# Memory attention of a transformer layer put into a written order, with the pre-norm weights in the folded keys

## The chip, the cores and the metric

The kernel runs on one core of a Trainium2 chip. The metric is the device time of one execution in microseconds (us). Before the change it is 1554.91 us (median of 3 runs, 1554.90 to 1556.88).

The core has five engines with a queue each: TensorE (PE: matrix products and transposes), VectorE (DVE), ScalarE (ACT), GpSimd (POOL) and SyncE (SP, which here issues the DMA transfers). Each engine works through its queue strictly in order, and waits on semaphores for the others. PE writes its results into PSUM, in which a tile of this kernel takes one bank. The banks go by four tags ("mm", "s", "tr", "pv") of two banks each.

## The reference, cut to what matters

```python
h = rmsnorm(x, g_mix_pre);  proj = h @ w_in                      # queries, keys, values, forget gates
y_fox = forgetting_attention(...); y_chk = chunked_relpos_attention(...)
y = concatenate([rmsnorm(y_fox, g_fox_out), rmsnorm(y_chk, g_chk_out)])
x = x + rmsnorm(y @ w_out, g_mix_post)                           # mixing
h = rmsnorm(x, g_mem_pre);  mem_n = rmsnorm(mem, g_mem_kv)
k = mem_n @ w_mk;  v = mem_n @ w_mv                              # 4 heads of 256, 256 memory tokens
p = softmax((h @ w_mq) k^T / 16)                                 # per head
x = x + rmsnorm((p v) @ w_mo, g_mem_post)                        # memory attention
h = rmsnorm(x, g_ff_pre)
x = x + rmsnorm(square(relu(h @ w_ff1)) @ w_ff2, g_ff_post)      # feed-forward, hidden 4096
```

There are 1024 rows of x, 1024 columns, everything is float32, and `rmsnorm(a, g)` divides a row by the root of its mean square (plus 1e-6) and multiplies by the weights g.

## The kernel before, in words

Products. A float32 product is made of three matmuls in a faster format (`mm3`, L102 to L104): each operand is split into a rounded part `hi` and the rest `lo`, and hi*hi, hi*lo and lo*hi are summed in PSUM. A weight block is loaded by DMA into a raw tile (`wraw`, three buffers), then split: `whi` by a copy on ACT (L96), `wlo` by a subtraction on DVE or POOL (L97). Activations are split in the same way when they are copied out of PSUM after a transpose (`to_T`: four transposes L127, `hi` on ACT L140, `lo` on DVE L141).

Tiling. Rows come in 8 blocks of 128 (`n`, or `b` within one half), the two halves of 512 rows are called `th`, the two halves of 512 output columns `nh`. A result of 128 rows by 512 columns sums 1024 products in 24 matmuls, or 512 products in 12.

Folding. The query and key projections of the memory attention are multiplied into one matrix ahead of time (`fold_keys`: `w_mq` of a head times the keys of that head, scaled by 1/16 at L460 and L462, stored to DRAM), so that scores are `h` times the folded keys. Likewise `fold_values` multiplies the memory values with `w_mo` (results `fv`, copied by L478 on DVE and L480 on ACT, stored to DRAM), so that the output is the probabilities times the folded values. Folded matrices are loaded back as weight blocks.

Stages around the change, in the order of time:
- End of attention (about 480 to 560 us). The last heads of the chunked attention run beside the memory keys (`mem_side`, `mkm`) and the folded keys (`fk`). In the same stretch `head_outputs(th, 0)` works on group 0 of the head outputs (the forgetting heads): load from DRAM (`oin`), `yT_hi` on ACT (L563), `yT_lo` on DVE (L564), squares on ACT (L567 to L570), sums of squares on DVE (L571, L572).
- Memory values (`mvm`, evacuated by `vm_hi` L442 and `vm_lo` L443) and the first half of the output projection, `mix_out((0, 1), 0)`: results `yw`, evacuated by L627 on ACT with the head's inverse root as scale. `head_rstd` makes that root from the summed squares by 4 small matmuls (`ssh`), DVE and POOL (L592).
- The second half of the output projection, `mix_out`, once for each `th`, with the weights loaded for each. A result is added (L629, DVE), squared with a sum for the row (`square_sum`, L597, ACT), and multiplied by the post-norm weights (L631, DVE). `close_block` then makes the inverse root of a row (L109 on DVE, L111 and L112 on POOL), adds the residual x (L673, DVE), stores the row, squares it (ACT), makes the next root and multiplies by that root and `g_mem_pre` (L678, DVE). `fold_values` runs in two parts between these.
- The transposes of the normed rows (`h2T`), scores, softmax (maximum L702 DVE, exponentials L704 ACT, reciprocal L706 DVE, scaling L709 POOL) and the transposed probabilities (`mtr` L712, `oT_hi` L715, `oT_lo` L716), for each `th` and each pair of heads: `cross`.
- The output of the memory attention (`ym`): `mem_out` for the first 512 columns, `row_tile` for the second. For `th` = 0 rows are closed as above with the names h3; the transposes of `h3T` lie in the middle of `mem_out` of `th` = 1 (`meanwhile`).
- The feed-forward: its weights are split ahead (`split_ahead`, `whi_a` L824, `wlo_a` L827), POOL makes eight sums `xf` (L894) of the parts of `h3T`, and the rows of `th` = 1 are closed one behind the other (`row_out`, `row_sum` L972, `row_norm` L979), then transposed (`trx` L914).

What sets the order. Up to the last stage the instructions of each engine are put in order by a scheduler, from the program's order, its own estimates of duration and the buffers. From `manual = ExitStack()` on, with `tc.manual_schedule()`, each engine gets its instructions in the order in which the program writes them. Before the change that begins at the last four row tiles.

Of the kernel before, what the change touches and what calls it, by code (L numbers as in the profile page):

```python
# [13 lines left out]
F32 = mybir.dt.float32  # L14
# [30 lines left out]
def build(ctx, tc, nc, out, t):  # L45
# [115 lines left out]
    gcol = const.tile([P, KC], F32, name="gcol")  # L161

# [271 lines left out]
    def mem_side(mT, src, name):  # L434

        act = Act(name, NM)
        for nb in range(KC):
            wh, wl = load_w(t[src][nb], [P, KC, P], lo_on=lo_eng())
            ps = mm_tile([P, NM], f"m{name}{nb}")
            for kc in range(KC):  # L440
                mm3(ps, wh[:, kc, :], wl[:, kc, :], mT.hi(kc), mT.lo(kc), kc == 0, kc == KC - 1)
            nc.scalar.activation(act.hi(nb), ps, AF.Copy)  # L442
            nc.vector.tensor_sub(act.lo(nb), ps, f(act.hi(nb)))  # L443
# [21 lines left out]
    def fold_values(vm, nhs):  # L465

        for nh in nhs:
            for h in range(4):
                wh, wl = load_w(row_pair(t["w_mo"], h, nh), [P, 2, HT], lo_on=lo_eng())
                g = u4(f"fvs{h}{nh}", (P, 2, HT), F32)  # L470
                for m in range(2):
                    ps = mm_tile([P, HT], f"fv{h}{nh}{m}")
                    ms = slice(m * P, (m + 1) * P)
                    for d in range(2):
                        mm3(ps, vm.hi(h * 2 + d, ms), vm.lo(h * 2 + d, ms), wh[:, d, :], wl[:, d, :],
                            d == 0, d == 1)
                    if m:
                        nc.vector.tensor_copy(g[:, m, :], ps)  # L478
                    else:
                        nc.scalar.activation(g[:, m, :], ps, AF.Copy)  # L480
                nc.sync.dma_start(vd_d[h][nh], g)
# [43 lines left out]
    nc.sync.dma_start(gcol, t["g_heads"])  # L525
    bias_rows()
# [24 lines left out]
    def head_outputs(th, g):  # L551
# [4 lines left out]
        for i in range(2):  # L556
            o = u4(f"oin{th}{g}{i}", (P, 2, HT), F32)
            for j in range(2):
                kc = g * 4 + i * 2 + j
                nc.sync.dma_start(o[:, j, :], od[kc][th])  # L560
                gc = gcol[:, kc:kc + 1]
                dh = yh[i][:, j, :]
                nc.scalar.activation(dh, o[:, j, :], AF.Copy, scale=gc)  # L563
                nc.vector.scalar_tensor_tensor(yl[i][:, j, :], o[:, j, :], gc, f(dh),  # L564
                                               op0=ALU.mult, op1=ALU.subtract)
# [9 lines left out]
    parts = {(th, 0): head_outputs(th, 0) for th in range(2)}  # L575
    fold_keys(mem_side(mT, "w_mk", "km"))
# [26 lines left out]
    PAIRS = ((0, 1), (2, 3))  # L603

    def mix_out(ths, g, after=None):

        rs = {}
        for nh in range(2):
            cs = slice(nh * HT, (nh + 1) * HT)
            ws = [load_w(row_pair(t["w_out"], 2 * g + i, nh), [P, 2, HT], u4 if g and nh else None,  # L610
                         lo_eng()) for i in range(2)]
            for th in ths:
                yh, yl, sq = parts[th, g]
                y, ss = ys[th]
                for b in range(4):
                    c = slice(b * P, (b + 1) * P)
                    ps = mm_tile([P, HT], f"yw{th}{g}{nh}{b}")
# [4 lines left out]
                    if th not in rs:  # L622
                        rs[th] = head_rstd(th, g, sq)
                    r = rs[th][:, b:b + 1]
                    yc = y[b][:, cs]
                    if g == 0:
                        nc.scalar.activation(yc, ps, AF.Copy, scale=r)  # L627
                    else:
                        nc.vector.scalar_tensor_tensor(yc, ps, r, yc, op0=ALU.mult, op1=ALU.add)  # L629
                        square_sum(yc, ss[b][:, nh:nh + 1], HT)  # L630
                        nc.vector.tensor_tensor(yc, yc, gpost[:, cs], op=ALU.mult)  # L631
            if after and nh in after:
                after[nh]()

    def o_at(o, b, kc):
        h, l = o[kc // 4][b // 2]
# [3 lines left out]
    def mem_out(th, o, y, ss, g, nhs=(0, 1), hook=lambda kp: None):  # L640


        for nh in nhs:
            cs = slice(nh * HT, (nh + 1) * HT)
            ps = [mm_tile([P, HT], f"ym{th}{nh}{b}", "mm" if b < 2 else "s") for b in range(4)]
            for kp in range(4):
                wh, wl = load_w(vd_d[kp][nh], [P, 2, HT], lo_on=lo_eng())
                for b in range(4):
                    for j in range(2):
                        mm3(ps[b], *o_at(o, b, kp * 2 + j), wh[:, j, :], wl[:, j, :],  # L650
                            kp == 0 and j == 0, kp == 3 and j == 1)
                hook(kp)
            for b in range(4):
                square_sum(ps[b], ss[b][:, nh:nh + 1], HT)
                nc.vector.tensor_tensor(y[b][:, cs], ps[b], g[:, cs], op=ALU.mult)

    def row_tile(o, b, wo, name, tag):

        ps = mm_tile([P, HT], name, tag)
        for kp in range(4):  # L660
            for j in range(2):
                mm3(ps, *o_at(o, b, kp * 2 + j), wo[kp][0][:, j, :], wo[kp][1][:, j, :],
                    kp == 0 and j == 0, kp == 3 and j == 1)
        return ps

    def close_block(y, ss, th, xin, xout, gnext, nm, bs):

        for b in bs:
            tb = th * 4 + b
            xt = p2.tile([P, D], F32, tag="xt", bufs=2, name=f"xt{nm}{tb}")  # L670
            nc.sync.dma_start(xt, xin(tb))
            r = rstd_of(ss[b], f"{nm}y{tb}")
            nc.vector.scalar_tensor_tensor(xt, y[b], r, xt, op0=ALU.mult, op1=ALU.add)  # L673
            nc.sync.dma_start(xout(tb), xt)
            s2 = small.tile([P, 1], F32, tag="ss", bufs=8, name=f"s2{nm}{tb}")
            square_sum(xt, s2)
            r = rstd_of(s2, f"{nm}x{tb}")
            nc.vector.scalar_tensor_tensor(y[b], xt, r, gnext, op0=ALU.mult, op1=ALU.mult)  # L678

    def turn(y, th, act, nm, pairs=PAIRS):  # L680
        for a, b in pairs:
            to_T(y[a], y[b], act, a * P, f"{nm}{th}{a}")

    def cross(th, act, after=None):

        o = []
        for nh in range(2):
            ps = [mm_tile([P, HT], f"ms{th}{nh}{b}", "mm" if b < 2 else "s") for b in range(4)]
            for kp in range(4):
                wh, wl = load_w(kd_d[kp][nh], [P, 2, HT], lo_on=lo_eng())  # L690
                for b in range(4):
                    c = slice(b * P, (b + 1) * P)
                    for j in range(2):
                        mm3(ps[b], act.hi(kp * 2 + j, c), act.lo(kp * 2 + j, c), wh[:, j, :], wl[:, j, :],
                            kp == 0 and j == 0, kp == 3 and j == 1)
            o.append([(u4(f"oT_hi{th}{nh}{i}", (P, 4, 2 * P)), u4(f"oT_lo{th}{nh}{i}", (P, 4, 2 * P)))
                      for i in range(2)])
            for b in range(4):
                st = small.tile([P, 6], F32, tag="mst", bufs=4, name=f"mst{th}{nh}{b}")
                pr = p2x.tile([P, 2, NM], F32, tag="mp", bufs=4, name=f"mp{th}{nh}{b}")  # L700
                sc = ps[b].rearrange("p (h m) -> p h m", h=2)
                nc.vector.tensor_reduce(st[:, 0:2], sc, axis=mybir.AxisListType.X, op=ALU.max, negate=True)  # L702
                for h in range(2):
                    nc.scalar.activation(pr[:, h, :], sc[:, h, :], AF.Exp, bias=st[:, h:h + 1],  # L704
                                         accum_out=st[:, 2 + h:3 + h])
                nc.vector.reciprocal(st[:, 4:6], st[:, 2:4])  # L706
                tr = mm_tile([P, 4, P], f"mtr{th}{nh}{b}", "tr")
                for h in range(2):
                    nc.gpsimd.tensor_scalar(pr[:, h, :], pr[:, h, :], st[:, 4 + h:5 + h], 1.0,  # L709
                                            op0=ALU.mult, op1=ALU.mult)  # L710
# [711 lines left out]
```

## Time and profile before

| | |
|---|---|
| Median of 3 runs | 1554.91 us |
| The profiled execution | 1553.97 us, of which the span from the first to the last instruction is 1552.2 us |
| PE (matmuls and transposes) busy | 1504.1 us, 97% of the span |
| DVE busy | 946.2 us, 61% |
| ACT busy | 796.5 us, 51% |
| POOL busy | 379.6 us, 24% |
| Mean granted PE clock | 0.993 |

Rows of the profile name the line, the engine, the operation and its operands as output<-input with the program's names; then come the count, the busy time with the mean duration in ns, and the idle time before with what ended it. A row of the waits tells which instruction ended PE's idle time: us in total, times, and the longest. A row of the timeline gives the start in us and the duration. Matmuls are pipelined, so that their mean duration is longer than the distance from one to the next.

### The profile page before, as it was taken

To read this page: it belongs to the slowest core of one execution; us is meant where nothing else is said; L and a number is where in the kernel's file an instruction comes from. 1 tells how busy PE (TensorE), PEld (TensorE's weight loads), DVE (VectorE), ACT (ScalarE), POOL (GpSimd) and SP (SyncE) were. 2 spreads that over 40 slices of the span, in tenths; PEclk is the share of its full clock that TensorE was granted. 3 is DMA by queue.
4 is the path that set the end of the run, shared out by engine and by line. 5 is a ranking of instruction groups with operands and counts; after the bars stand their busy time and mean duration, and the time that the engine had idled before them with its cause. 6 is when DMAs were issued, how large, how long until landed. Compare 5 with 4: busy or idle time off the path is not lost.

```text
span 1552.2 us, 22221 instructions
## 1 busy us (share of the span) xinstructions
PE 1504.1 (97%) x7948; PEld 1276.3 (82%) x7948; DVE 946.2 (61%) x1612; ACT 796.5 (51%) x1409; POOL 379.6 (24%) x546
## 2 busy tenths in 40 slices
PE   8999999999998999999999989999999999999998
PEld 7978889789877998777888877888888888888886
DVE  6366574665467763478655568766555474746577
ACT  5356564565466663545454445555555544444442
POOL 4234351343233440002220250443323000000021
PEclk9999999999999899999999999999999999999999
DMA  5132140242223375267524454775444595535565
GB/s 214 50 95 65 52 113 23 76 146 64 55 65 128 93 236 195 82 217 257 190 82 139 147 176 139 249 250 189 155 151 149 185 390 192 174 109 195 198 244 190
DMA packets 90640, 237.49 MB, mean 153 GB/s; under 512 B 10505, under 2 KB 18705, under 8 KB 90530
## 3 DMA queue, kind: packets, MB, share of 16 engines
q1 hardware_dynamic: 90530, 236.08, 45.7%
q8 instruction: 63, 1.03, 0.3%
q14 instruction: 47, 0.39, 0.1%
HBM read 168.35 MB, written 59.30 MB: 147 GB/s over the span
## 4 chain that ended last, share of the span: by engine, by line
PE 84%; DVE 6%; ACT 3%; DMA 3%; issue 2%; POOL 2%; SPq 0%; DVEq 0%; POOLq 0%; ACTq 0%
PE fx L103 4%; PE fx L104 4%; PE fx L102 3%; PE fy L104 3%; PE fy L103 3%; PE fy L102 3%; PE px L104 3%; PE px L103 3%; PE px L102 3%; PE ms L104 2%; PE ms L103 2%; PE ms L102 2%; PE v L102 2%; PE pz L103 2%; PE pz L104 2%
## 5 line engine op out<-in xcount | busy, mean ns | idle before, releaser
L96 ACT ACTIVATE whi<-wraw 128x1024 fp32r<-128x1024 f32 x92 | 96.8, 1057 | 97.0 <-PE ms L104 29.2
L97 DVE TENSOR_TENSOR wlo<-wraw,whi 128x1024 fp32r<-128x1024 f32 x68 | 84.3, 1244 | 75.0 <-ACT whi L96 74.5
L1149 ACT ACTIVATE whif<-ra 128x1024 fp32r<-128x1024 f32 x37 | 39.2, 1060 | 122.4 <-PE fy L103 62.6
L1151 DVE TENSOR_TENSOR wlof<-ra,whif 128x1024 fp32r<-128x1024 f32 x37 | 45.3, 1225 | 91.2 <-ACT whif L1149 91.2
L1265 POOL TENSOR_SCALAR rf<-sf 128x1 f32<-128x1 f32 x8 | 8.3, 1036 | 326.4 <-ACT jf L1250 326.1
L102 PE MATMUL v<-whiv,hT_hi 128*128 128x256 f32 (+1 forms) x256 | 73.7, 288 | 0.8 <-DVE vs L238 0.8
L103 PE MATMUL v<-wlov,hT_hi 128*128 128x256 f32 (+1 forms) x256 | 73.4, 287 | 0.0
L104 PE MATMUL v<-whiv,hT_lo 128*128 128x256 f32 (+1 forms) x256 | 73.2, 286 | 0.0
L97 POOL TENSOR_TENSOR wlo<-wraw,whi 128x1024 fp32r<-128x1024 f32 x24 | 58.1, 2422 | 48.0 <-ACT whi L96 26.9
L103 PE MATMUL fx<-vlof,whif 128*128 128x512 f32 x168 | 65.4, 389 | 0.0
L102 PE MATMUL fx<-vhif,whif 128*128 128x512 f32 x168 | 65.4, 389 | 0.0
L104 PE MATMUL fx<-vhif,wlof 128*128 128x512 f32 x168 | 65.4, 389 | 0.0
L1039 POOL TENSOR_TENSOR sc<-wf,wf 128x512 f32<-128x512 f32 x14 | 21.2, 1513 | 143.5 <-DMA wf<-in_w_ff 127.2
L102 PE MATMUL yw<-whi,yT_hi 128*128 128x512 f32 x128 | 50.4, 397 | 2.6 <-ACT yw L627 1.4
L102 PE MATMUL ym<-whi,oT_hi 128*128 128x512 f32 x128 | 49.6, 402 | 3.0 <-DVE h3T_lo L141 3.0
L103 PE MATMUL yw<-wlo,yT_hi 128*128 128x512 f32 x128 | 50.2, 393 | 1.7 <-DVE wlo L97 1.7
L103 PE MATMUL ym<-wlo,oT_hi 128*128 128x512 f32 x128 | 50.8, 397 | 0.0
L104 PE MATMUL ym<-whi,oT_lo 128*128 128x512 f32 x128 | 50.7, 396 | 0.0
L103 PE MATMUL ms<-wlo,h2T_hi 128*128 128x512 f32 x128 | 50.4, 393 | 0.0
L102 PEld LDWEIGHTS v<-whiv,hT_hi 128*128 128x128 f32 x256 | 49.2, 192 | 1.2 <-DVE vs L238 1.0
L104 PE MATMUL yw<-whi,yT_lo 128*128 128x512 f32 x128 | 50.0, 390 | 0.0
L104 PE MATMUL ms<-whi,h2T_lo 128*128 128x512 f32 x128 | 49.9, 393 | 0.0
(752 smaller groups left out, 5160.0 us busy)
## 6 DMA issues: line engine op xcount, KB each, us to landing
ra<-gd SPq DMA_DIRECT2D x56, 512.0 KB, 3.8
wg<-in_w_ff SPq DMA_DIRECT2D x56, 512.0 KB, 6.1
wf<-in_w_ff SPq DMA_DIRECT2D x38, 512.0 KB, 3.8
gd<-s SPq DMA_DIRECT2D x48, 256.0 KB, 2.1
wraw<-in_w_qk SPq DMA_DIRECT2D x16, 512.0 KB, 3.8
wraw<-wk SPq DMA_DIRECT2D x16, 512.0 KB, 3.7
wraw<-wv SPq DMA_DIRECT2D x16, 512.0 KB, 3.5
gd<-u SPq DMA_DIRECT2D x32, 256.0 KB, 2.1
```

What stands on the lines that cost most here:

```text
L96: nc.scalar.activation(hi, raw, AF.Copy)
L97: (lo_on or nc.gpsimd).tensor_sub(lo, raw, f(hi))
L102: nc.tensor.matmul(ps, lh, rh, start=start, stop=False, skip_group_check=more)
L103: nc.tensor.matmul(ps, lh, rl, start=False, stop=False, skip_group_check=more)
L104: nc.tensor.matmul(ps, ll, rh, start=False, stop=stop, skip_group_check=more)
L1039: eng.tensor_sub(sc[:, k1], r0[:, k0], r1[:, k0])
L1149: nc.scalar.activation(ah, ra, AF.Copy)
L1151: nc.vector.tensor_sub(al, ra, f(ah))
L1265: nc.gpsimd.tensor_scalar(r, ssf[b][:, 0:1], ssf[b][:, 1:2], EPS, op0=ALU.add, op1=ALU.add)
```

## The change

Four things are changed, all between the end of attention and the feed-forward.

1. Pre-norm weights in the folded keys. `g_mem_pre` is loaded as columns (`gmcol`) and multiplied into the folded keys, in place of 1/16, which moves to the memory keys. A result of 128x512 is now evacuated as two of 128x256, one on ACT and one on DVE, each with its column of weights. The normed row needs only its root: `normed` is a copy with a scale on ACT, where it was a multiplication by root and weights on DVE.
2. `head_outputs` of group 0 is split: the loads stay ahead of the memory keys, the arithmetic is written behind `fold_keys`, ahead of the memory values.
3. The written order begins at the second half of the output projection. `mix_tile` makes row block `n` of column half `nh`; the weights of that half (`wq`) are split once for both `th`. Around it `add`, `gained`, `res` and `normed` of this row block and the ones before are written in a fixed order. `tick()` counts parts of a result, and `at(delay, call)` puts work a number of ticks later: the transposes, the scaling of the probabilities, the closing of rows. `Stream` loads weight blocks up to three ahead and splits them at fixed places. Inverse roots of a pair of half-row sums are made on POOL alone (`inverse_rms`), without the small DVE sum.
4. The two folds of the values stand among the scores: scores (0, 0), fold 0, scores (0, 1), scores (1, 0), fold 1, scores (1, 1). The transposes of `h3T` are spread over the ticks of the first output half of `th` = 1, and the splits of the feed-forward weights and POOL's sums (`part`) are written inside the loop over the last four row tiles.

The number and the shapes of the matmuls are the same.

```diff
-    parts = {(th, 0): head_outputs(th, 0) for th in range(2)}
-    fold_keys(mem_side(mT, "w_mk", "km"))
+    o_in = {(th, 0): load_outputs(th, 0) for th in range(2)}
+    fold_keys(mem_side(mT, "w_mk", "km", 0.0625))
...
-                    if kp:
-                        nc.vector.tensor_scalar(g, ps, 0.0625, None, op0=ALU.mult)
-                    else:
-                        nc.scalar.activation(g, ps, AF.Copy, scale=0.0625)
+                    for a in range(2):
+                        gc = gmcol[:, mh * 4 + kp * 2 + a:mh * 4 + kp * 2 + a + 1]
+                        if a:
+                            nc.vector.tensor_scalar(g[:, a, :], ps[:, a, :], gc, None, op0=ALU.mult)
+                        else:
+                            nc.scalar.activation(g[:, a, :], ps[:, a, :], AF.Copy, scale=gc)
...
+    parts = {(th, 0): head_outputs(th, 0, o_in[th, 0]) for th in range(2)}
+    vm = mem_side(mT, "w_mv", "vm")
+    ys = [y_tiles("w", th) for th in range(2)]
+    mix_first()
+    for th in range(2):
+        parts[th, 1] = head_outputs(th, 1, load_outputs(th, 1))
+    wq = [[load_w(row_pair(t["w_out"], 2 + i, nh), [P, 2, HT], u4 if nh else p2q, nc.vector)
+           for i in range(2)] for nh in range(2)]
+    manual = ExitStack()
+    manual.enter_context(tc.manual_schedule())
...
+    def turns(xa, xb, act, c0, name):
+        def call(k):
+            tr = mm_tile([P, 2, 2, P], f"tr_{name}_{k}", ("tr", "pv")[k // 2 % 2])
+            for j in range(2):
+                for q in range(2):
+                    nc.tensor.transpose(tr[:, j, q, :], (xa, xb)[q][:, (k + j) * P:(k + j + 1) * P], ident)
+            ...
+            nc.scalar.activation(dh, src, AF.Copy)
+            nc.vector.tensor_sub(act.l[i][:, o:o + 2, c0:c0 + 256], src, f(dh))
+        return [lambda k=k: call(k) for k in range(0, KC, 2)]
...
+    def normed(n):
+        nc.scalar.activation(ys[n // 4][0][n % 4], xr[n], AF.Copy, scale=rr[n])
...
+    for n in range(8):
+        if n + 1 < 8:
+            x_in(n + 1)
+        if n in (1, 2):
+            st.split(n)
+        if n in (4, 6):
+            turn_rows(0, n - 4, (1, 3, 5, 7))
+        ps = mix_tile(n, 0)
+        if n % 4 == 0:
+            r1[n // 4] = head_rstd(n // 4, 1, parts[n // 4, 1][2])
+        add(n, 0, ps)
+        if n:
+            gained(n - 1, 1)
+            res(n - 1)
+        if n > 1:
+            normed(n - 2)
+        gained(n, 0)
+        ps = mix_tile(n, 1)
+        add(n, 1, ps)
+        root(n)
...
+    turn_rows(1, 0, (2, 4, 6, 8))
+    at(1, lambda: (gained(7, 1), res(7)))
+    at(2, lambda: normed(6))
+    at(5, lambda: normed(7))
+    turn_rows(1, 2, (9, 11, 13, 15))
+    scores(0, 0, S00)
+    gffpre = gain(p2, t["g_ff_pre"], "g_ff_pre")
+    fold_values(0, V0)
+    scores(0, 1, S01)
+    scores(1, 0, S10)
+    fold_values(1, V1)
+    scores(1, 1, S11)
...
+    for a, spots in ((0, (2, 4, 6, 8)), (2, (9, 10, 12, 14))):
+        for d, call in zip(spots, turns(ym[0][a], ym[0][a + 1], h3, a * P, f"h3{a}")):
+            at(d, call)
...
     for b in range(4):
-        ps = row_tile(o, b, wo, f"ym11{b}", "tr" if b < 2 else "pv")
+        for i in (0, 2):
+            part(i + b % 2, b // 2)
+        ps = row_tile(1, b, Y1)
+        if b < 3:
+            row_out(4 + b, ps)
         if b:
-            row_sum(b - 1)
-            row_norm(b - 1)
+            row_sum(3 + b)
+            if b < 3:
+                at(2, lambda b=b: row_norm(3 + b))
+            else:
+                row_norm(6)
         if b < 3:
+            split_ahead(b, raws.pop(b), b == 0)
             raws[EARLY + b] = ff1_raw(EARLY + b)
-            residual_in(b + 1)
-            row_out(b, ps)
+            residual_in(5 + b)
```

More of the change, by code (lines that the diff above doesn't have):

```diff
@@ L632, in mix_out @@
[L632 to L636, printed above, removed]
-        c = slice(b % 2 * P, (b % 2 + 1) * P)
-        return h[:, kc % 4, c], l[:, kc % 4, c]
[L640 to L655, printed above, removed]
@@ new lines, in build, with at, tick @@
+    mix_first()
+    for th in range(2):
+        parts[th, 1] = head_outputs(th, 1, load_outputs(th, 1))
[3 more added lines that the diff above has]
+    manual.enter_context(tc.manual_schedule())
+    clock, due = [0, 0], []
+    def at(delay, call):
+        clock[1] += 1
+        due.append((clock[0] + delay, clock[1], call))
+        due.sort(key=lambda e: e[:2])
+    def tick():
+        clock[0] += 1
+        while due and due[0][0] <= clock[0]:
+            due.pop(0)[2]()
@@ new lines, in build @@
+    x_in(0)
+    for n in range(8):
+        if n + 1 < 8:
[17 more added lines that the diff above has]
+        root(n)
@@ new lines, in row_norm @@
+    def row_norm(n):
+        nc.vector.scalar_tensor_tensor(ym[n // 4][n % 4], xts[n], rx[n], gffpre, op0=ALU.mult, op1=ALU.mult)
+    ym[0], ssm[0] = y_tiles("m", 0)
+    first_half(0, Y0, ym[0], ssm[0], (4, 6, 7, 8))
+    residual_in(0)
+    for n in range(4):
+        ps = row_tile(0, n, Y0)
+        row_out(n, ps)
+        if n:
+            row_sum(n - 1)
+            at(2, lambda n=n: row_norm(n - 1))
+        residual_in(n + 1)
+        if n in (0, 2):
+            st.split(Y1 + 1 + n // 2)
@@ L764, in build @@
+    at(1, lambda: row_sum(3))
+    at(3, lambda: row_norm(3))
     p2xs.close()
-    y, ss = y_tiles("m", 1)
+    ym[1], ssm[1] = y, ss = y_tiles("m", 1)
     NP = FF // (2 * P)
@@ L866, in split_ahead @@
             h.raw, h.hi, h.lo = raw, u4(f"wah{j}", (P, D)), u4(f"wal{j}", (P, D))
-            was[j] = h.both(lo_eng())
+            was[j] = h.both(nc.vector)
         else:
```

387 lines of the change are left out of this document (216 added, 171 removed).

## The prediction

> **What bounds the kernel now.** I read the page first, for the engine that is nearly always busy.
>
> ```profile
> span 1552.2 us, 22221 instructions
> PE 1504.1 (97%) x7948; PEld 1276.3 (82%) x7948; DVE 946.2 (61%) x1612; ACT 796.5 (51%) x1409; POOL 379.6 (24%) x546
> ```
>
> TensorE (PE) is the bound, and its matmuls stay the same in number and shape. So the change can only add or remove time in which PE stands or runs at the half clock. The table by stage says how much there is; its columns are length, then PE, weight load, DVE, ACT and POOL busy, granted clock, DMA share, GB/s.
>
> ```profile
> 480.00:580.00 100.00, 92.99 (x713) 88.99 (x712) 73.37 (x179) 71.32 (x140) 44.82 (x74) 0.95 0.51 161
> 506.00:516.00 10.00, 8.35 (x34) 7.15 (x34) 9.51 (x24) 9.58 (x20) 3.88 (x8) 0.51 0.32 111
> 580.00:660.00 80.00, 74.83 (x423) 64.37 (x422) 30.28 (x40) 37.34 (x54) 2.02 (x2) 1.00 0.42 145
> 660.00:740.00 80.00, 75.94 (x337) 59.49 (x336) 63.96 (x81) 41.79 (x75) 11.90 (x22) 1.00 0.68 237
> 740.00:880.00 140.00, 140.00 (x669) 116.24 (x668) 76.54 (x106) 63.45 (x137) 30.63 (x56) 1.00 0.42 136
> 880.00:920.00 40.00, 36.02 (x162) 29.54 (x161) 25.55 (x28) 19.08 (x33) 17.50 (x16) 0.91 0.45 156
> 900.00:910.00 10.00, 7.00 (x22) 5.53 (x23) 6.96 (x8) 3.50 (x7) 9.16 (x5) 0.66 0.40 152
> 920.00:980.00 60.00, 58.28 (x271) 47.58 (x270) 47.31 (x64) 31.30 (x52) 11.35 (x14) 1.00 0.55 186
> 1000.00:1100.00 100.00, 100.00 (x443) 82.81 (x442) 63.12 (x80) 53.22 (x79) 36.77 (x27) 1.00 0.61 209
> ```
>
> The last row is the price of work: 100/443 = 0.226 us for a 512-column matmul. Hence 12 of them, one 128x512 result of the mixing, take 2.72 us, and a row block of two results 5.45.
>
> The loss of before, stage by stage, is idle time plus busy time lost to the clock. A, end of attention (480:580): 7.0 idle and, in 506:516, 8.35 x 0.49 = 4.1, together 11.1. B, memory values and first half of the output projection: 5.2. C, second half, mixing and first fold: 4.1 (PE's modelled ends cover part of short gaps, so somewhat more). D, scores: 0. E, second output half: 4.0 idle and 7.00 x 0.34 = 2.4 at the low clock, 6.4. F, start of the feed-forward: 1.7. All of it is 28.5 us: no order of this stretch can win more. Who ends PE's waits:
>
> ```profile
> PE pvc5g L390 <- DVE plc5g L384: 3.0, 2, 2.6
> PE ym L102 <- DVE h3T_lo L141: 3.0, 1, 3.0
> PE mvm L102 <- ACT whi L96: 1.8, 1, 1.8
> PE yw L102 <- DVE yw L629: 1.0, 1, 1.0
> PE px L102 <- ACT whi_a L824: 1.1, 1, 1.1
> ```
>
> **A and B: the head outputs of group 0 move.** Before, their scaling and squares run inside the end of attention; after, only their loads stay there, and ACT and DVE get the work in one block behind the last folded key, ahead of the first memory values.
>
> ```profile
> L564 DVE SCALAR_TENSOR_TENSOR yT_lo<-oin,gcol,yT_hi 128x512 fp32r<-128x512 f32 x8 | 8.6, 1075 | 0.5 <-ACT yT_hi L563 0.5
> L563 ACT ACTIVATE yT_hi<-oin,gcol 128x512 fp32r<-128x512 f32 x8 | 5.7, 714 | 1.2 <-DMA oin<-od 1.2
> 500.77 2.78 DVE L564 SCALAR_TENSOR_TENSOR yT_lo<-oin,gcol,yT_hi 128x512 fp32r<-128x512 f32 x1
> 595.73 0.37 ACT L442 ACTIVATE vm_hi<-mvm 128x256 fp32r<-128x256 f32 x1
> 598.61 0.37 ACT L442 ACTIVATE vm_hi<-mvm 128x256 fp32r<-128x256 f32 x1
> ```
>
> In A the 2.78 us instruction stands ahead of the `plc5g` that PE waits for, and the half clock follows the hole. With some 9 us less on either queue I expect A's loss to go from 11.1 to about 4 (waits on DMA and POOL in the softmax stay): 7 won. The ends are 1 (other work fills the hole) and 11 (all of it).
>
> In B one memory value takes 598.61 - 595.73 = 2.88 us of PE. They go through two banks, so PE stands after 5.8 us from the first matmul on until `vm_hi(0)` and `vm_lo(0)` have emptied a bank. ACT has ahead of that 8 `yT_hi` (5.7), 4 squares of 512 columns (0.63), one of 1024 (1.06) and two `whi` (1.06): 11.4; DVE has 8 `yT_lo` ((8.6 - 2.78)/7 = 0.83 without the disturbed one), two `wlo` (1.25) and 4 adds (0.69, as for other 512-column operations below): 11.9. Neighbours on a queue overlap by some 0.08, so the bank is free near 12 to 13: a hole of about 6.8 in place of the 1.8 that the late weights cost there: 5 lost (ends: 2, if the block starts before the last key; 9, with a low clock behind it).
>
> **C: the mixing in written order.** Second-half weights are split once for both halves (four `whi`, four `wlo` and four loads fewer), the multiplication by the pre-norm weights goes into the folded keys, and `normed` moves from DVE (L678) to ACT. The first fold leaves for D. What counts is the chain between DVE and ACT, each strictly in order.
>
> ```profile
> L96 ACT ACTIVATE whi<-wraw 128x1024 fp32r<-128x1024 f32 x48 | 50.3, 1057 | 51.4 <-PE ms L104 29.2 <-DMA wraw<-in_w_out 6.6 <-DMA wraw<-wv 5.3
> L97 DVE TENSOR_TENSOR wlo<-wraw,whi 128x1024 fp32r<-128x1024 f32 x48 | 59.6, 1249 | 39.9 <-ACT whi L96 39.6
> L629 DVE SCALAR_TENSOR_TENSOR yw<-yw,rs,yw 128x512 f32<-128x512 f32 x16 | 11.8, 745 | 1.3 <-PE yw L104 1.3
> L597 ACT ACTIVATE junk<-yw 128x512 bf16<-128x512 f32 x16 | 10.0, 626 | 17.6 <-DVE yw L629 17.6
> L597 ACT ACTIVATION_READ_ACCUMULATOR junk<-yw 128x1 f32 x16 | 3.0, 188 | 0.0
> L597 ACT ACTIVATE junk<-xth 128x1024 bf16<-128x1024 f32 x16 | 16.9, 1055 | 30.0 <-DVE xth L673 21.8 <-DVE xth L972 8.1
> L673 DVE SCALAR_TENSOR_TENSOR xth<-yw,h2y,xth 128x1024 f32<-128x1024 f32 x8 | 10.3, 1282 | 2.6 <-POOL h2y L112 2.6
> L140 ACT ACTIVATE h2T_hi<-tr_h 128x512 fp32r<-128x512 f32 x16 | 9.1, 594 | 9.3 <-PE tr_h L127 9.0
> L961 POOL TENSOR_SCALAR h3y<-ssm 128x1 f32<-128x1 f32 x4 | 2.5, 632 | 5.4 <-ACT junk L597 5.4
> L962 POOL TENSOR_TENSOR h3y<-h3y,mhalf 128x1 f32<-128x1 f32 x4 | 2.2, 562 | 0.3
> 717.29 0.68 DVE L631 TENSOR_TENSOR yw<-yw,g_mix_post 128x512 f32<-128x512 f32 x1
> 717.89 0.69 DVE L141 TENSOR_TENSOR h2T_lo<-tr_h,h2T_hi 128x512 fp32r<-128x512 f32 x1
> 491.11 0.44 PE tr_mem L127 x4
> ```
>
> Starts on DVE lie 0.6 apart for 0.68 of work, so I take 0.08 off each duration in a row. Let s(n) be the start of the square of row block n's second half, and PE start at 0. s(0) is 7.4: two results, the head roots and one add. Then, while blocks are split, DVE does `wlo` behind ACT's `whi`, an add, a gain, `res`, a gain and an add: 0.8 + 1.1 + 1.2 + 0.65 + 0.6 + 1.2 + 0.6 + 0.65 = 6.7, so s(1) = 14.1. With `normed` ahead of the next square on ACT it is 7.6: s(2) = 21.7. `normed(1)` ends after square and root (0.63 + 0.19 + 0.63 + 0.56 = 2.0), `res` 1.2, its square 1.2 and itself 1.06: 21.7 + 5.5 = 27.2. PE asks for it at its first transposes, in block 4 after six matmuls: 4 x 5.45 + 1.36 = 23.2. A hole of 3.8.
>
> From block 4 on the chain of one block is square 0.58, transposed copy 0.59, `h2T_lo` 0.6, add 0.65, gain 0.6, `res` 1.2, square 1.1, `normed` 1.06, copy 0.59, `h2T_lo` 0.6, add 0.65: with the hand-overs 8.6, where PE needs 5.45 + 2 x 0.44 = 6.3. So PE is stopped again where it wants `normed(3)` (block 6, about 3.8) and `normed(5)` (in the scores, about 3.2): 10.8 in all. Against 4.1 idle before that is 6.7 more; part of before's short gaps is hidden under modelled ends, so I take 5 lost (ends: 4 won with no hole, 8 lost).
>
> **D: folds among the scores.** PE waits for nothing in D before. Now the fold's results alternate on two banks, and ACT's copies of them queue behind the exponentials of the scores just done.
>
> ```profile
> L704 ACT ACTIVATE mp<-ms,mst 128x256 f32<-128x256 f32 x32 | 14.8, 473 | 6.9 <-DVE mst L702 6.7
> L480 ACT ACTIVATE fvs<-fv 128x512 f32<-128x512 f32 x8 | 4.7, 593 | 2.0 <-PE fv L104 2.0
> ```
>
> Eight exponentials are 8 x 0.47 = 3.8 us, and read-outs of 0.2 each come with them: some 4.8 in a row, against two fold results of 1.36 each on PE. That is up to 2.1 at the first fold and little at the second. I take 2 lost (0 to 4).
>
> **E: the transposes of the first feed-forward operand** stand in a bunch among the second half's matmuls before; written out, they come one to a tick of 1.36 us, with no weight split between `h3T_hi` and `h3T_lo`. 6.4 falls to 1: 5.4 won (ends 3 and 6.4).
>
> **F: the last four row tiles** now have the feed-forward splits inside the loop (they ran ahead of it before), and the eight POOL sums.
>
> ```profile
> L972 DVE SCALAR_TENSOR_TENSOR xth<-ym,h3y,xth 128x1024 f32<-128x1024 f32 x4 | 5.1, 1284 | 0.9 <-POOL h3y L962 0.9
> L827 DVE TENSOR_TENSOR wlo_a<-wf,whi_a 128x1024 fp32r<-128x1024 f32 x4 | 5.5, 1364 | 0.0
> L894 POOL TENSOR_TENSOR xf<-h3T_hi,h3T_lo 128x512 f32<-128x512 f32 x8 | 14.0, 1768 | 13.1 <-DVE h3T_lo L141 12.8
> ```
>
> One tile's chain is a multiplication 0.6, `row_sum` 1.2, its square 1.06, `whi_a` 1.06, `wlo_a` 1.3 and `row_norm` 1.2, with hand-overs 6.8 against PE's 5.45. After three tiles `row_norm(5)` ends 3.4 after PE asks for it in the transposes: 3.4 lost (0 to 6). POOL's roots wait behind one sum of 1.77 at most.
>
> **At nothing:** 16 evacuations of folded keys become 32 of half the size (0.37 each by the `vm_hi` rows, on two engines at once); eight small sums of two squares leave DVE, the shorter way to the root; the column weights' load lies on SP's queue ahead of long attention work; x rows are asked for a block ahead of their use and land in under 5.45. Should a store that waits for `res` hold back SP, the next load has a block's cover.
>
> **Sum:** +7 - 5 - 5 - 2 + 5.4 - 3.4 = -3.0, that is 3 us slower. The profiled execution took 1553.97 (1.8 beside its span); 1557.0 is my number. The median of the runs shown stands 0.9 higher.
>
> **Rivals.** (1) Faster: the chain of DVE and ACT never stops PE. It is decided at one place, `normed(1)` before 23.2 on the walk above, 4 us sooner; the hand-overs and the two splits there are what could shrink. Then C wins 4 instead of losing 5 and F, the same kind of chain, loses nothing: 3 slower becomes 9.4 faster, 1544.6. For it speaks that DVE is only 64 of 80 us busy in C before; against it that this is a chain, not a load. (2) Each new hole also costs clock. In 506:516 and 900:910 a hole was followed by a low clock that cost 4.1 and 2.4; at 2.4 for B and two holes of C it is 7 more: 1564. The Trainium skill ("TensorE: Matmul & The Clock Gate", Part 1: The HAM clock gate) has the clock fall to half after an idle window of about 3.4 us, and Part 4 there has transposes not count as busy. By that the holes of 3.8 in front of transposes would each pay about 1.7, an estimate from that page; the two low-clock rows agree with a fall behind a hole, and no row here shows the case with transposes. (3) The move from A gives nothing there, since attention's other waits take the place: 1553.97 + 10 = 1564.
>
> **Chances.** The forecast's own case (1552 to 1561) 0.42, half of it within 0.2% (3.1 us, about what a measurement can tell from no change) and half slower; rival 1 0.28; rival 2 0.19; rival 3 0.11. Faster 0.28, same 0.21, slower 0.51. The range goes from rival 1 to a little past rival 2: 1545 to 1567.
>
> **What would show it.** In the profile after: A without the 2.6 wait on `plc5g` and a clock near 1.00; one wait of the third memory value of 6 to 8 us on `vm_lo`; transposes `h2T` waiting three times for `normed` (ACT), 3 to 4 us each; the row of E full; transposes `trx` waiting about 3 us for `row_norm`. The forecast is wrong if the first stays, or if C's three waits are missing, or if the clock column is under 0.95 in B or C.

## The result and the profile after

The changed kernel takes 1563.61 us (median of 5 runs, 1561.20 to 1564.28), against 1554.91 us for the kernel before (median of 5, 1553.11 to 1556.88). The ratio is 1.0052 with an interval of 1.0038 to 1.0067: about 8 us slower. The profiled execution has a span of 1561.1 us. First the page of the changed kernel:

```profile
span 1561.1 us, 22175 instructions
PE 1504.4 (96%) x7948; PEld 1279.6 (82%) x7948; DVE 935.0 (60%) x1596; ACT 800.7 (51%) x1421; POOL 374.0 (24%) x546
```

PE is busy for as long as before (1504.4 against 1504.1), so nearly all of the difference of the spans, 8.9 us, is time in which PE stands. (The busy time holds the work done at a low clock, before as after.) DVE has 11 us less to do, and that did not make the kernel faster. The table by stage of the changed kernel, with the columns of the prediction's table (the windows are set to the stages of this kernel, so that A and B begin earlier, and the lengths differ):

```profile
470.00:560.00 90.00, 89.37 (x696) 86.15 (x696) 62.86 (x169) 63.26 (x132) 41.54 (x77) 1.00 0.50 161
560.00:660.00 100.00, 92.28 (x518) 80.88 (x517) 50.32 (x70) 52.81 (x83) 7.65 (x6) 0.97 0.49 159
575.00:585.00 10.00, 6.09 (x30) 6.04 (x31) 7.28 (x13) 5.20 (x9) 1.41 (x1) 0.66 0.44 160
660.00:740.00 80.00, 69.91 (x321) 56.11 (x319) 45.78 (x63) 43.67 (x88) 16.68 (x37) 0.94 0.38 125
670.00:680.00 10.00, 5.78 (x22) 4.81 (x21) 3.76 (x6) 3.79 (x8) 2.75 (x6) 0.66 0.73 232
740.00:880.00 140.00, 138.79 (x642) 114.76 (x642) 68.74 (x90) 60.25 (x120) 18.19 (x39) 1.00 0.44 151
880.00:900.00 20.00, 18.72 (x94) 15.24 (x93) 14.27 (x15) 11.10 (x17) 5.13 (x6) 1.00 0.72 232
900.00:980.00 80.00, 69.77 (x309) 56.82 (x308) 59.18 (x73) 35.69 (x66) 19.66 (x22) 0.94 0.42 149
930.00:940.00 10.00, 7.18 (x29) 6.15 (x30) 7.66 (x9) 3.30 (x7) 4.43 (x5) 0.70 0.44 159
```

| stage | PE idle before, us | PE idle after, us | lowest clock before | lowest clock after |
|---|---|---|---|---|
| A, end of attention | 7.0 | 0.6 | 0.51 | 1.00 |
| B, memory values, first output half | 5.2 | 7.7 | 1.00 | 0.66 |
| C, mixing | 4.1 | 10.1 | 1.00 | 0.66 |
| D, scores and folds | 0 | 1.2 | 1.00 | 1.00 |
| E, output of the memory attention | 4.0 | 1.3 | 0.66 | 1.00 |
| F, last row tiles, start of the feed-forward | 1.7 | 10.2 | 1.00 | 0.70 |
| sum | 22.0 | 31.1 | | |

The clock of a stage is that of its lowest row in the two tables. The sums of idle time differ by 9.1 us, near the 8.9 of the spans. A and E were won, as the change lets one expect; B, C and F lost more. PE's waits in the changed kernel (us in total, times, longest) name three places:

```profile
PE tr_h L671 <- ACT yw L752: 9.2, 4, 4.2
PE trx L1080 <- DVE ym L918: 7.1, 1, 7.1
PE ssh L583 <- DVE sq L565: 5.3, 1, 5.3
PE px L104 <- DVE wlo_a L1001: 2.0, 2, 1.5
PE ym L103 <- DVE wlo L97: 1.3, 1, 1.3
```

`tr_h` behind `yw` L752 is C: transposes that wait for `normed` on ACT. `trx` behind `ym` L918 is F: transposes that wait for `row_norm` on DVE. `ssh` behind `sq` is B: PE's queue stands at the head sums, which need the squares of the block written behind the folded keys. PE's next two instructions there are these:

```profile
578.58 1.84 PE L583 MATMUL ssh<-o,sq 128*128 128x1 f32 x8 [5.31 <-DVE sq L565]
580.75 0.58 PE L102 MATMUL mvm<-mT_hi,whi 128*128 128x256 f32 x1 [0.33 <-DVE vm_lo L444]
```

The second is the third memory value. It still has to wait for `vm_lo` to empty its bank, so that the wait for a bank lies behind the wait for the squares: 7.5 us pass between the end of the second memory value (573.27) and the third, and the head sums fall into them.

The timeline of C in the changed kernel (start, duration) has the chain of the prediction. First ACT with `normed` (L752) of rows 1, 3, 4 and 5, then DVE's wait for the transposed copy:

```profile
673.64 1.13 ACT L752 ACTIVATE yw<-xm,h2x 128x1024 f32<-128x1024 f32 x1
...
693.75 1.13 ACT L752 ACTIVATE yw<-xm,h2x 128x1024 f32<-128x1024 f32 x1
...
702.55 1.14 ACT L752 ACTIVATE yw<-xm,h2x 128x1024 f32<-128x1024 f32 x1
...
711.36 1.13 ACT L752 ACTIVATE yw<-xm,h2x 128x1024 f32<-128x1024 f32 x1
```

```profile
676.39 0.69 DVE L676 TENSOR_TENSOR h2T_lo<-tr_h,h2T_hi 128x512 fp32r<-128x512 f32 x1 [2.64 <-ACT h2T_hi L675]
```

From row 3 on each block takes 8.8 us (693.75, 702.55, 711.36), against the 6.3 that the prediction reckons for PE. The transposes wait 4.2 us up to 674.83, 2.2 up to 694.93 and 2.5 up to 712.54.

F has something that the prediction did not have. The groups of DVE between 900 and 945 us, and the timeline of DVE and of POOL in the changed kernel:

```profile
L918 DVE SCALAR_TENSOR_TENSOR ym<-xth,h3x,g_ff_pre 128x1024 f32<-128x1024 f32 x3 | 5.9, 1958 | 2.2 <-POOL h3x L685 2.2
L1001 DVE TENSOR_TENSOR wlo_a<-wf,whi_a 128x1024 fp32r<-128x1024 f32 x2 | 4.6, 2304 | 4.5 <-ACT whi_a L998 4.5
L1001 DVE TENSOR_TENSOR wal<-wf,wah 128x1024 fp32r<-128x1024 f32 x1 | 1.2, 1227 | 0.3 <-ACT wah L998 0.3
```

```profile
928.28 2.29 DVE L1001 TENSOR_TENSOR wlo_a<-wf,whi_a 128x1024 fp32r<-128x1024 f32 x1 [2.22 <-ACT whi_a L998]
930.49 2.28 DVE L918 SCALAR_TENSOR_TENSOR ym<-xth,h3x,g_ff_pre 128x1024 f32<-128x1024 f32 x1
```

```profile
928.23 1.26 POOL L1062 TENSOR_TENSOR xf<-h3T_hi,h3T_lo 128x512 f32<-128x512 f32 x1
929.44 2.24 POOL L1062 TENSOR_TENSOR xf<-h3T_hi,h3T_lo 128x512 f32<-128x512 f32 x1
```

The same split takes 1.23 us once and 2.30 twice, and `row_norm` 2.28 where it took 1.28 before. The slow ones lie beside POOL's two sums, 928.23 to 931.68. But the fast split, the first of the three, lies beside a sum too:

```profile
911.11 1.23 DVE L1001 TENSOR_TENSOR wal<-wf,wah 128x1024 fp32r<-128x1024 f32 x1 [0.26 <-ACT wah L998]
911.14 2.34 POOL L1062 TENSOR_TENSOR xf<-h3T_hi,h3T_lo 128x512 f32<-128x512 f32 x1
```

Here DVE began 0.03 us ahead, and it is POOL's sum that takes 2.34 in place of 1.26. In the rows before, POOL began first and ended at 929.49, DVE's split 1.08 later (930.57), POOL's second sum 1.11 after that (931.68), and `row_norm` 1.09 after that (932.77). The rows read as if the two engines took turns: whichever begins second waits until the other is done.

### The profile page after: what moved, and what is told of

The parts are those of the page before. It is cut to its first block, busy times and chain, and to the rows that moved or that the text cites. A ratio compares the mean times of both kernels' runs of the same rounds, so it can differ in the third digit from the quotient of the medians.

```text
span 1561.1 us, 22175 instructions
## 1 busy us (share of the span) xinstructions
PE 1504.4 (96%) x7948; PEld 1279.6 (82%) x7948; DVE 935.0 (60%) x1596; ACT 800.7 (51%) x1421; POOL 374.0 (24%) x546
## 5 line engine op out<-in xcount | busy, mean ns | idle before, releaser
L96 ACT ACTIVATE whi<-wraw 128x1024 fp32r<-128x1024 f32 x88 | 92.7, 1057 | 82.2 <-PE qc L103 13.3
L97 DVE TENSOR_TENSOR wlo<-wraw,whi 128x1024 fp32r<-128x1024 f32 x64 | 79.5, 1246 | 83.9 <-ACT whi L96 83.4
L102 PE MATMUL ms<-whi,h2T_hi 128*128 128x512 f32 x128 | 51.2, 400 | 0.5 <-DVE yw L731 0.5
```

What stands on the lines that cost most here:

```text
L96: nc.scalar.activation(hi, raw, AF.Copy)
L97: (lo_on or nc.gpsimd).tensor_sub(lo, raw, f(hi))
L102: nc.tensor.matmul(ps, lh, rh, start=start, stop=False, skip_group_check=more)
```

## The experiments

All are made from the changed kernel by the edits shown, and their times are given by the ratio to the kernel before, which ran on the same chip beside them. On that scale the changed kernel is 8.1 us above the kernel before.

**The head outputs back in attention.**

```diff
     o_in = {(th, 0): load_outputs(th, 0) for th in range(2)}
+    parts = {(th, 0): head_outputs(th, 0, o_in[th, 0]) for th in range(2)}
     fold_keys(mem_side(mT, "w_mk", "km", 0.0625))
```

> The arithmetic of the group-0 head outputs is put back ahead of the memory keys, all else as in the changed kernel. Theory: the move itself won at the end of attention (loss of PE there about 11 us less) and lost before the memory values (wait for the summed squares 5.3 us, and a low clock behind it). Then this run is slower than the changed kernel by about 6 us (1569 to 1571), shows waits on plc and spc of the chunked attention again and no wait of the summed squares over 1 us. Rival: attention's end got better through other parts of the change (folded keys in halves, scale in the memory keys); then this run is about 5 us faster than the changed kernel (1558 to 1560).

Measured: 1567.11 us, ratio 1.0079 (1.0064 to 1.0094), some 4 us slower than the changed kernel, whose interval overlaps this one by a little (1.0067 and 1.0064). Attention's waits are back, and the wait of the squares is gone from the list:

```profile
PE pvc5g L390 <- ACT phc5g L384: 4.0, 2, 2.0
PE pvc5g L391 <- DVE plc5g L385: 3.4, 2, 2.1
```

So it is the move that relieved attention, not the other parts of the change. The size is under the 6 expected: the 7.4 us of these two rows come back, and 5.3 at the squares go.

**The head outputs spread over the memory values.** In written order, behind each memory value's evacuation, comes one piece (an `hi` copy and squares on ACT; its `lo` and adds on DVE one value later).

```diff
+    with tc.manual_schedule():
+        pieces = head_pieces(0, 0, o_in[0, 0]) + head_pieces(1, 0, o_in[1, 0])
...
+            nc.scalar.activation(vm.hi(nb), ps, AF.Copy)
+            nc.vector.tensor_sub(vm.lo(nb), ps, f(vm.hi(nb)))
+            for call in los:
+                call()
...
+            for h, _ in now:
+                h()
+            los = [l for _, l in now]
```

> The same arithmetic stays behind the folded keys, but in written order one piece per memory value, behind the evacuation of that value. Theory: the hole of 5.3 us and the low clock behind it come from the evacuation of the first memory values queueing behind the whole block on ACT and DVE; both go, and the time falls by 5 to 7 us to about 1557. Rival: ACT and DVE are simply short of time in this stage; then the hole is cut up into waits of the later memory values or of the first mixing results, and the time falls by less than 2 us.

In this run one of the squares overwrites rows that a later `lo` still reads, so that this low part is not the reference's; the instructions are the same in kind and number. Measured: 1556.72 us, ratio 1.0015 (1.0006 to 1.0025), 5.7 us faster than the changed kernel. What is left there:

```profile
PE mvm L104 <- DVE wlo L97: 2.4, 2, 1.7
PE mvm L102 <- ACT whi L96: 0.7, 1, 0.7
```

The hole of 5.3 us was a matter of order. Two orders change in this run, and it does not tell them apart: the block is spread, and the first head sums come later (589.42 us, at the start of the seventh memory value; 578.58 in the changed kernel, behind the second). Shortage on DVE shows too, as 3 us of waits for weight splits, but not enough for the rival.

**POOL's sums replaced by copies.**

```diff
             nc.scalar.activation(dh, src, AF.Copy)
             nc.vector.tensor_sub(act.l[i][:, o:o + 2, c0:c0 + 256], src, f(dh))
+            if also:
+                also(i, src)                 # xf[i, a] <- src, on ACT
...
-        for i in (0, 2):
-            part(i + b % 2, b // 2)
```

> POOL's eight sums (1.77 us each) of the parts of h3T go; ACT copies the same values from PSUM at the transposes instead. Theory: beside these sums DVE's two-input instructions take twice their time (wlo_a and row_norm 2.3 instead of 1.25 us) and POOL's roots wait for them; without them row_norm is back at 1.28 us, the wait of the transposes trx for row_norm falls from 7.1 to about 3 us and the time by 4 to 6 us, to about 1558.5. Rival: the chain of splits and norms in the loop makes the hole whatever POOL does; then the wait stays at 6 to 7 us and the time within 1.5 us.

Measured: 1561.42 us, ratio 1.0045 (1.0030 to 1.0060). The groups of DVE at the same place, and PE's waits, in this run:

```profile
L920 DVE SCALAR_TENSOR_TENSOR ym<-xth,h3x,g_ff_pre 128x1024 f32<-128x1024 f32 x3 | 3.8, 1281 | 2.2 <-POOL h3x L687 2.2
L1011 DVE TENSOR_TENSOR wlo_a<-wf,whi_a 128x1024 fp32r<-128x1024 f32 x2 | 2.5, 1225 | 4.4 <-ACT whi_a L1008 4.4
```

```profile
PE px L104 <- DVE wlo_a L1011: 3.1, 2, 2.6
PE trx L1083 <- DVE ym L920: 2.8, 1, 2.8
PE ym L102 <- ACT whi L96: 1.5, 1, 1.5
```

The theory holds for the durations: 2.30 goes to 1.23, 1.96 to 1.28, the hole from 7.1 to 2.8. On the time the run decides nothing: its interval and that of the changed kernel overlap. Part of the 4.3 us of the hole is given back: the next weight split is waited for 3.1 us in place of 2.0, and 1.5 come in where a split of the memory output is late. In all, PE's idle time between 880 and 980 us falls from 11.5 to 8.3. What became of these 3.3 us is not shown by the times.

**`normed` ahead of two squares on ACT.**

```diff
     for n in range(8):
...
+        if n > 1:
+            at(2, lambda n=n: normed(n - 2))
         ps = mix_tile(n, 0)
...
             res(n - 1)
-        if n > 1:
-            normed(n - 2)
         gained(n, 0)
```

> In the mixing, normed of two row blocks back stands ahead of the squares of the current block on ACT, instead of behind the residual's square. Theory: the transposes wait because of the order on ACT (the root is there one chain earlier); the first wait falls from 4.2 us to under 1, all four together from 9.2 to 3 to 5 us, and with the low clock the time falls by 5 to 8 us to about 1557. Rival: the turn-around of DVE and ACT per block (8.8 us against 6.3 on PE) is what limits; then the waits only move to the later transposes, their sum stays over 7 us and the time falls by less than 2 us.

Measured: 1553.34 us, ratio 0.9994 (0.9985 to 1.0004): level with the kernel before, 9 us faster than the changed kernel. Of the transposes' wait for `normed` 0.2 us is left. One wait has come in its place:

```profile
PE ms L102 <- DVE yw L731: 3.0, 1, 3.0
```

The first scores wait for the last mixing results to leave their bank: the backlog of DVE and ACT is seen where PE runs out of banks, but once, not at every turn. A block still takes 7.8 us (`normed` at 684.06, 691.83 and 699.59). The gain was above the range given, since much of the low clock behind the holes went with them (0.98 over the stage, 0.94 in the changed kernel).

**The turn-around shortened too.** `normed` as above, and

```diff
             nc.scalar.activation(dh, src, AF.Copy)
-            nc.vector.tensor_sub(act.l[i][:, o:o + 2, c0:c0 + 256], src, f(dh))
+            at(2, lambda: nc.vector.tensor_sub(act.l[i][:, o:o + 2, c0:c0 + 256], src, f(dh)))
...
     x_in(0)
+    for th in range(2):
+        r1[th] = head_rstd(th, 1, parts[th, 1][2])
     for n in range(8):
```

> As the run with normed ahead of the squares (1553.3), and besides the low parts of the turned rows are subtracted two ticks later on DVE, and both head roots are made ahead of the first row block. Theory: what is left of the mixing's loss is the turn-around of DVE and ACT per block (8.8 us against PE's 6.3), seen as the 3.0 us that the first scores wait for the last mixing result to leave its bank; without DVE standing behind each transposed copy the turn-around is under 6.5 and that wait goes: 3 to 5 us less than 1553.3, about 1549.5. Rival: the backlog comes from the start of the mixing (roots and weight splits of the first two blocks), and the later subtraction changes nothing: at most 1.5 us less.

Measured: 1548.20 us, ratio 0.9962 (0.9947 to 0.9977), 5 us less than with `normed` alone. The stage of C is nearly full in this run:

```profile
660.00:740.00 80.00, 78.09 (x383) 64.42 (x382) 58.24 (x78) 53.67 (x101) 16.81 (x38) 1.00 0.49 174
```

PE does 383 matmuls in these 80 us, where the changed kernel does 321, and a block takes 5.4 to 6.4 us (`normed` at 675.01, 680.55, 685.98 and 692.36). The edit changes the subtraction and the roots together, so their shares are not told apart.

**`normed` back on DVE**, in the same place of the order.

```diff
     def normed(n):
-        nc.scalar.activation(ys[n // 4][0][n % 4], xr[n], AF.Copy, scale=rr[n])
+        nc.vector.tensor_scalar(ys[n // 4][0][n % 4], xr[n], rr[n], None, op0=ALU.mult)
```

> Only the engine of normed is changed back: DVE makes it, in the same place of the written order, as a multiplication by the root. Theory: normed is late because on ACT it stands behind the residual's square (1.06 and 0.19 us) which itself waits for DVE; on DVE it follows res at once, so the first transposes wait 1.5 to 2.5 us instead of 4.2, and the time falls by 2 to 5 us. Rival: DVE becomes the longer queue of the two and the waits stay or grow; the time is the changed kernel's 1563.6 or above.

Measured: 1556.21 us, ratio 1.0015 (1.0005 to 1.0024), 5.8 us faster than the changed kernel. The waits of the transposes:

```profile
PE tr_h L671 <- DVE yw L752: 3.5, 3, 2.4
```

From 9.2 to 3.5, and the longest from 4.2 to 2.4; the gain is a little above the 2 to 5 expected. Of the change's parts, then, the one that took work from DVE, `normed` on ACT, was the dear one where it was put: what DVE had less to do there was worth less than the 6 us that the place behind the residual's square cost.

**The last row tiles.** The copies of the sums as above, ahead of the subtraction; and

```diff
     for b in range(4):
+        if b < 3:
+            at(3, lambda b=b: split_ahead(b, raws.pop(b), b == 0, los))   # whi_a only
         ps = row_tile(1, b, Y1)
...
             row_sum(3 + b)
-            if b < 3:
-                at(2, lambda b=b: row_norm(3 + b))
-            else:
-                row_norm(6)
         if b < 3:
-            split_ahead(b, raws.pop(b), b == 0)
+            los.pop()()                                                 # wlo_a
+        if b:
+            row_norm(3 + b)
+        if b < 3:
             raws[EARLY + b] = ff1_raw(EARLY + b)
```

> As the run with the sums copied by ACT (1561.4), with the copy ahead of the subtraction, and in the last row tiles the rounded half of a weight split is made before the tile ends, the rest between row_sum and row_norm. Theory: the remaining wait of the transposes trx (2.8 us) is the chain of one tile, 6.4 us between row_norm and row_norm against 5.45 on PE, because the split stands in it; out of the chain the wait falls under 0.7 us, and the time by 3 to 5 us to about 1557.5. Rival: the late start at the first tile (weights of the feed-forward land late) sets it; then the wait stays over 2 us and the time within 1.5 us of 1561.4.

Measured: 1556.72 us, ratio 1.0015 (1.0005 to 1.0025), 5.8 us faster than the changed kernel and 4.7 less than with the copies alone.

```profile
PE px L104 <- DVE wlo_a L1011: 3.1, 2, 2.6
PE ym L103 <- DVE wlo L97: 1.2, 1, 1.2
...
PE trx L1088 <- DVE ym L920: 0.7, 1, 0.7
```

The wait for `row_norm` is 0.7, and that of 1.5 for a split of the memory output is gone. So the order in this loop was the rest of the hole; the run moves the halves of the split, `row_norm` and the copies together, and their shares are not told apart. The next splits of the feed-forward still make PE wait 3.1.

**All three places.**

> The three places together on the changed kernel: head outputs one piece per memory value (minus 7 in its own run; here no square runs ahead of a read), the mixing as in the run of this call (minus 10 by normed alone, 13 to 14 with the rest) and the last tiles as in the run of this call (minus 5 to 6). If the places are independent, as PE's waits suggest, the time is 1563.6 - 7 - 13.5 - 5.5 = 1537.6, 17 us under the kernel before. Rival: part of each gain is given back at the next stage because its feeders are then late (the weight loads, DVE near the feed-forward); then it ends at 1544 to 1548.

Measured: 1535.92 us, ratio 0.9881 (0.9866 to 0.9896): 18 us faster than the kernel before, 27 faster than the changed one. The page and the stages:

```profile
span 1532.2 us, 22193 instructions
PE 1494.3 (98%) x7948; PEld 1272.3 (83%) x7948; DVE 926.1 (60%) x1596; ACT 804.6 (53%) x1429; POOL 358.3 (23%) x538
```

```profile
480.00:560.00 80.00, 79.38 (x642) 77.37 (x641) 59.82 (x164) 59.91 (x126) 39.29 (x70) 1.00 0.55 176
560.00:660.00 100.00, 95.76 (x551) 83.58 (x550) 53.77 (x75) 57.37 (x89) 11.14 (x13) 1.00 0.50 168
660.00:740.00 80.00, 78.09 (x383) 64.42 (x382) 55.62 (x74) 50.88 (x96) 15.21 (x34) 1.00 0.51 185
740.00:880.00 140.00, 139.08 (x649) 114.73 (x648) 68.84 (x88) 63.32 (x128) 18.78 (x40) 1.00 0.43 147
880.00:960.00 80.00, 75.01 (x344) 61.08 (x343) 58.48 (x78) 40.05 (x72) 13.01 (x20) 1.00 0.50 175
```

The three places are independent within the noise: 5.7 + 14 + 5.8 = 25.5 us alone, 26.6 together. PE itself is busy 10 us less than in the changed kernel, for the same 7948 matmuls; none of these stages has a low clock any more. The change's plan was good, and its order at three places was not.

## Why the prediction was right, and where it was not

The number, 1557.0, is 6.6 us under the median. The direction was right and the time lies inside the range, but above the forecast's own case (1552 to 1561) and on the number of the second rival, 1564. The forecast's own sign against itself, a clock under 0.95 in B or C, is met in C (0.94). Counted as the prediction counts (idle time, and busy time lost in the row of the lowest clock), the change lost 8.9 us where 3.0 were forecast:

| step | forecast, us | counted after, us |
|---|---|---|
| A | 7 won | 10.5 won |
| B | 5 lost | 4.6 lost |
| C | 5 lost | 8.0 lost |
| D | 2 lost | 1.2 lost |
| E | 5.4 won | 5.1 won |
| F | 3.4 lost | 10.7 lost |

Low clock outside these rows is not counted, so C and F lost somewhat more. That A won more than forecast hides part of what C and F lost more; that much of the agreement is luck. By its steps:

- **A** was forecast at 7 won, with 4 left. PE's idle time fell from 7.0 to 0.6 and the low clock went. The mechanism was the one given (putting the work back brings `plc5g` and `phc5g` waits of 7.4 us), and its gain was undersized: the waits that were to stay, of the softmax on DMA and POOL, are hardly left.
- **B** was forecast as a hole of 6.8 us. The hole is 5.3 and is ended by the squares; the wait for the bank that was forecast lies behind it, and the third memory value starts 13.5 us after the first, where 12 to 13 was forecast. So the walk through the queues held. That the stage lost about the 5 forecast is partly luck: idle time rose by only 2.5, and a low clock (0.66), which the term left out, added 2.1.
- **C** was walked through the queues, and the walk held: a turn-around of 8.6 was forecast and 8.8 measured; three holes of 3.8, 3.8 and 3.2 us were forecast, and 4.2, 2.2 and 2.5 came at the three places named. The idle time rose by 6.0, where 5 was the term, and the low clock behind the first hole, which the term left out, added 2.0 in its row alone. That the order on ACT, not the load, was the cause, is shown by the run with `normed` ahead of the squares: it has the same instructions.
- **D** was forecast at 2 lost; idle time rose by 1.2, among the folds.
- **E** was forecast at 5.4 won; idle time and low clock together fell from 6.4 to 1.3, that is 5.1.
- **F** is the step that failed. The forecast was 3.4 lost, by a chain of 6.8 us with `wlo_a` at 1.3 and `row_norm` at 1.2. The wait was 7.1 and idle time rose by 8.5. The chain was right (without POOL's sums the hole is 2.8), the durations were not: behind POOL's sums these two instructions take 2.30 and 2.28 us. The row of `xf` was quoted, and only its effect on POOL's own roots was counted. The price of 1.3 was itself a mean over such cases: in the kernel before, two of these splits ran beside the sums and took 1.32 and 1.71 us, as they began 0.2 and 0.6 us before a sum ended. The Trainium skill states the rule ("GPSIMD Engine Reference", 1. Specifications: GpSimd's SBUF interfaces are shared with VectorE, with contention for instructions of two SBUF inputs). The trace agrees: in the rows of F the instruction that begins second takes about 1.1 us longer, be it DVE's or POOL's. The profile before had a sign of it too: the `yT_lo` of 2.78 us, which I took as a disturbance without asking for its cause, began at 500.77 us beside this row of POOL's timeline, and ended 0.55 after it.

```profile
500.26 2.74 POOL L97 TENSOR_TENSOR wlo<-wraw,whi 128x1024 fp32r<-128x1024 f32 x1 [0.16 <-POOL biasc L309]
```

Some sums of the prediction are slightly off: the terms given as 6.7 add up to 6.8, 27.2 less 23.2 is a hole of 4.0 and not 3.8, and a chain of 6.8 against 5.45 gives 2.7 us over two tiles or 4.1 over three, not 3.4. Against the 10.7 lost in F these are small.

Of the rivals, the first did not come, since `normed(1)` was late by the 4 us of the walk. The second came in part, and its time is the measured one: a low clock stood behind the holes of B and F and the first of C, and not behind the other two of C, where the holes of 2.2 and 2.5 us were followed by a clock of 1.00. As F's hole was mis-sized too, the agreement of the number proves nothing. The clock is the reason why closing a hole was worth more than the hole: with `normed` ahead of the squares, 9.0 us of the transposes' waits went and a wait of 3.0 came, and the time fell by 9. The third did not come.

## What to carry to other kernels

When an order is written by hand, walk each in-order queue once through a steady round and hold the turn-around between two engines, not the load of either, against what PE needs: 8.8 us against 6.3 in the changed kernel, 7.8 with one instruction moved ahead of two squares, which was worth 9 us, and about PE's time with the last edit. Moving an instruction to the engine with less to do gains nothing when it lands behind a wait there. Price an instruction by the neighbours that it will have, and ask which of the two begins first: DVE's subtractions and multiplications of two SBUF operands nearly doubled when they began just behind one of POOL's sums, and lost nothing when they began just ahead of it.

## What the runs showed of the hardware that was not expected

The first is DVE beside POOL. A split of 128x1024 takes 2.30 us when it begins 0.05 us after POOL's sum, and 1.23 when it begins 0.03 us before it; then POOL's sum takes 2.34 in place of 1.26. A multiplication of the same size takes 2.28 against 1.28. Without the sums, all of them are fast (1.23 and 1.28).

The second is the clock behind short holes. The Trainium skill ("TensorE: Matmul & The Clock Gate", Part 1: The HAM clock gate) has the clock fall after an idle window of about 3.4 us. Here shorter waits had a low clock behind them: after one of 2.4 us in the run with `normed` on DVE, the clock of the next 7 us is 0.65:

```profile
674.00:681.00 7.00, 6.26 (x23) 5.28 (x24) 3.97 (x8) 2.68 (x6) 2.67 (x5) 0.65 0.66 225
```

Nor does the length of the wait decide it: the changed kernel's wait of 2.5 us in C had none. And the same wait, 2.6 us for `wlo_a` at the start of the feed-forward, had a clock of 0.53 behind it in the run of the last row tiles and 1.00 in the run of all three places:

```profile
950.00:957.00 7.00, 6.57 (x16) 5.23 (x17) 6.91 (x11) 2.79 (x5) 0.00 (x0) 0.53 0.64 225
```

```profile
928.00:935.00 7.00, 6.49 (x33) 5.48 (x34) 6.91 (x11) 3.28 (x7) 0.00 (x0) 1.00 0.70 228
```

PE got through 16 matmuls in the one and 33 in the other. In the clock records of the traces here the low stretches between 470 and 980 us last 3.41, 6.83 or 10.24 us, one, two or three times the same length. A free-running window, as that page has it, would make such a difference by where the hole falls in it; no run here was made to show that.
